# A decoder kernel on one core: decode scores in four column groups, and three half output products moved into the fourth head's attention

## Chip, core and metric

The kernel runs on one core of one Trainium2 chip. Its time is the device time of one execution in microseconds (us); shorter is better. The engines are named as in the profile: PE (TensorE matmul) and PEld (its weight loads), DVE (VectorE), ACT (ScalarE), POOL (GpSimd) and SP (SyncE, which issues most transfers). Each engine works through its own queue in order.

## What is computed

The reference is one decoder layer for a prompt of 1024 tokens and for 8 decode sequences of one new token each, whose 256 earlier keys and values lie in a paged cache. Cut to what matters:

```python
xp = xp + merge_groups(oa, o_r, gr, subln, lam_init) @ w_out      # prompt: attention and retention
# decode, for the 8 sequences:
k_past = cache_k[page_table]                                       # 2 pages of 128 keys each
k_all = concatenate([k_past, ka_d], axis=1)                        # and the new key: 257
def probs(qi, ki):                                                 # for each half of q and k
    s = einsum('bqhd,bkhd->bhqk', qi, ki) * scale + bias
    return softmax(where(mask, s, neg))
attn = probs(q1, k1) - lam * probs(q2, k2)                         # 4 heads, two softmaxes each
oa_d = einsum('bhqk,bkhd->bqhd', attn, v_all)
```

Retention, a memory attention, a squared-ReLU MLP and the norms follow or stand beside this.

## The kernel before

All float32 products of the body are made of two parts: a number is split into a high part in the type fp32r and the rest, and `mm3` issues three matmuls for each term (high by high, high by low, low by high). Activations lie transposed, 128 channels by 1032 tokens (1024 of the prompt and 8 of decode), in `UH` and `UL`, rows 0 to 7; products work on `CH` = 344 tokens at a time, so c = 0, 1, 2. Weight blocks ("units") come by one DMA of 512 KB each into a buffer `raw` and are split by ACT (high part, L128) and DVE (low part, L129).

Prompt attention runs head by head. PE's order is written out by hand there (`pin`): a loop over g = -4 to 39 whose body is a list `todo` for item g (head g // 10): `turn(g + 1)` transposes a block of probabilities (L78, then ACT `ah` L1049 and DVE `al` L1050), `scores` makes two score products for each bank (tile `sp`) which DVE adds to the mask and reduces (L1016), ACT exponentiates (L1022) and DVE combines (L1031), and `weigh(g)` multiplies by the values (tile `av`). Scores of the next head are made from its place 5 on, so from g = 33 there are none. Between the pieces of `todo` stand steps of a generator called filler: for heads 0 to 2 the projection of the next head; for the fourth head (g = 28 to 39) the decode steps, so many at each g as `DFILL` says.

`decode_steps` (from L1149) first fetches cached key pages (`fetch`, 256 KB each, two to a step; tile `ck`), builds a block-diagonal query `qblkd` and then makes 16 score products of 64 columns (4 heads x 8 sequences x 2 halves) by 512 cached keys of all four heads in tile `dsc`; `hm` picks the right head's 128 of them in eight DVE operations (L1229). A bias product (`dbias`) and the new token's own score (`down`) come between. Softmax over 64 rows, a combination product (`dcomb`, L1241) and a way through DRAM (`atd`, `at`) give the weights that the decode values need later. Twelve empty steps keep the combination behind g = 39.

`operand_steps` brings the retention half of the output projection's operand into rows 4 to 7 of UH and UL (L1266, DMAs of 2064 KB from OPH and OPL, issued by POOL), and the heads' outputs into rows 0 to 3. They are called at the g of `OPERAND_AT`. `out_ahead` begins the output projection inside the loop: at g = 37, 38 and 39 four steps each of three matmul terms' worth, the first four terms (rows 4 to 7) of the products (0,0), (0,1), (1,0), where (ft, c) is an output block of 128 channels and a third of the tokens. The remaining steps stand behind the loop. Four units of its weights are loaded at g = 32 (`LOADS_AT`) and split at the g of `UNITS_AT`.

`proj_residual` (L1439) then does the other products: for ft = 0 to 7 the first two thirds of the tokens, 24 matmuls each, DVE adding the residual from the `x` rows (L1459), ACT and POOL summing squares; then the last thirds, five of them begun (`stage`) while the decode values are finished, since these tokens include the decode ones. `fetch` there brings the x rows and weight units. The memory queries (tile `mq`) follow.

## Time and profile before

| what | value |
| --- | --- |
| time, median of 3 runs | 1483.44 us (1481.57 to 1485.17) |
| profiled execution | 1483.49 us |
| its span, first to last instruction | 1481.7 us |
| PE busy | 1468.0 us (99%), 10917 matmul records |
| DVE busy | 1097.3 us (74%) |
| ACT, POOL busy | 677.6 us (46%), 305.6 us (21%) |
| chain that ended last | PE 90%, DVE 5%, ACT 2% |
| DMA | 236.69 MB, mean 160 GB/s |

Busy time is the union of an engine's instructions. A matmul's record includes the time until its results are through, so the records of neighbouring matmuls overlap, and the distance between two starts tells what one costs. The time in brackets behind a row of the timeline is how long the engine was idle before it, and who released it. Times within the span are counted from its first instruction.

### The profile page before, as it was taken

Reading aid. Unit: us, or ns where it says so; the run is one execution under the profiler, and the core shown is the slowest. Engines: PE = TensorE matmul, PEld = TensorE weight load, DVE = VectorE, ACT = ScalarE, POOL = GpSimd, SP = SyncE. Lnnn points to the kernel's source line nnn. Section 1 sums busy time; section 2 is a strip of 40 time slices with the busy share of each in tenths; the row PEclk is TensorE's granted clock in tenths of the full one; section 3 lists DMA queues with packets and bytes.
Section 4 is the critical chain, followed back from the end, with each engine's and each line's share of the span. In section 5 each row is a group of like instructions: output and inputs, shape, how many; then the busy total and the mean of one; then the engine's idle time right before and its main releaser. Section 6 shows DMA issues by size and latency. Waiting matters only on the chain.

```text
span 1481.7 us, 27906 instructions
## 1 busy us (share of the span) xinstructions
PE 1468.0 (99%) x10917; PEld 1399.2 (94%) x10917; DVE 1097.3 (74%) x2265; ACT 677.6 (46%) x1328; POOL 305.6 (21%) x331
## 2 busy tenths in 40 slices
PE   9999999999999999999999999999999999999998
PEld 7899779999679999989999999999999999999998
DVE  7666536888768545567877987888888888787876
ACT  6534435666552341258536544333434443343454
POOL 0035333122214311106022000000001311110380
PEclk9999999999999999999999999999999999999998
DMA  8255738214846177474582443334446774536273
GB/s 288 68 187 169 205 70 190 72 34 143 253 145 242 68 247 189 118 237 109 179 299 69 157 148 131 141 137 157 158 144 211 239 252 143 172 102 194 79 130 115
DMA packets 125784, 236.69 MB, mean 160 GB/s; under 512 B 13654, under 2 KB 75787, under 8 KB 125524
## 3 DMA queue, kind: packets, MB, share of 16 engines
q1 hardware_dynamic: 90826, 174.52, 37.2%
q0 software_dynamic: 23632, 40.60, 10.2%
q10 hardware_dynamic: 11194, 19.78, 3.6%
q8 instruction: 86, 1.41, 0.4%
q14 instruction: 46, 0.38, 0.1%
HBM read 170.24 MB, written 57.52 MB: 154 GB/s over the span
## 4 chain that ended last, share of the span: by engine, by line
PE 90%; DVE 5%; ACT 2%; issue 1%; DMA 1%; ACTq 0%; POOL 0%; SPq 0%; DVEq 0%
PE dn L2345 21%; PE Z L2177 9%; PE qkp L75 7%; PE pr_o L75 6%; PE mq L75 6%; PE pr_m L75 6%; PE X L2177 6%; PE Y L2177 6%; PE grp L75 3%; PE sp L75 2%; PE av L75 2%; PE mv L75 2%; PE mk L75 1%; PE mpv L75 1%; PE vap_z L522 1%
## 5 line engine op out<-in xcount | busy, mean ns | idle before, releaser
L2345 PE MATMUL dn<-UH,wd 128*128 128x258 f32 (+1 forms) x1800 | 325.9, 283 | 0.9 <-DVE c L2479 0.8
L2345 PEld LDWEIGHTS dn<-UH,wd 128*128 128x128 f32 x1800 | 278.7, 189 | 1.8 <-DVE c L2479 0.8
L2345 PE MATMUL dn<-UL,wd 128*128 128x258 f32 x900 | 253.9, 282 | 0.0
L2345 PEld LDWEIGHTS dn<-UL,wd 128*128 128x128 f32 x900 | 169.7, 189 | 0.1
L2479 DVE TENSOR_TENSOR c<-c,dn 128x258 f32<-128x258 f32 (+1 forms) x217 | 88.8, 417 | 36.7 <-PE dn L2345 34.2
L2203 ACT ACTIVATE hq<-r 128x258 f32<-128x258 f32 x128 | 53.7, 421 | 118.0 <-DVE r L2202 117.9
L2177 PE MATMUL Z<-T_h,wu 128*128 128x258 f32 x512 | 98.1, 283 | 0.0
L2177 PE MATMUL X<-UH,wu 128*128 128x258 f32 x512 | 97.5, 282 | 0.0
L2321 ACT CAST wd<-raw_d 128x512 fp32r<-128x512 f32 x96 | 58.7, 619 | 79.6 <-PE dn L2345 74.1
L1985 ACT CAST wu<-raw_up 128x512 fp32r<-128x512 f32 x96 | 59.0, 616 | 61.0 <-PE Z L2177 53.2
L2314 ACT CAST UH<-raw_h 128x1032 fp32r<-128x1032 f32 x56 | 58.7, 1055 | 53.3 <-PE dn L2345 27.7
L2177 PEld LDWEIGHTS X<-UH,wu 128*128 128x128 f32 x512 | 81.3, 188 | 0.0
L2177 PEld LDWEIGHTS Z<-T_h,wu 128*128 128x128 f32 x512 | 81.3, 189 | 0.0
L2315 DVE TENSOR_TENSOR UL<-raw_h,UH 128x1032 fp32r<-128x1032 f32 x56 | 73.7, 1315 | 8.4 <-ACT UH L2314 8.4
L2322 DVE TENSOR_TENSOR wd<-raw_d,wd 128x512 fp32r<-128x512 f32 x96 | 72.2, 758 | 10.3 <-ACT wd L2321 10.3
L2214 POOL DMA_DIRECT2D HT<-ht x32 | 17.1, 536 | 292.0 <-DVE ht L2213 271.6
L2177 PE MATMUL Z<-T_l,wu 128*128 128x258 f32 x256 | 72.3, 282 | 0.0
L2177 PE MATMUL X<-UL,wu 128*128 128x258 f32 x256 | 72.3, 282 | 0.0
L128 ACT CAST wh_u<-raw_u 128x1024 fp32r<-128x1024 f32 x43 | 44.5, 1048 | 57.3 <-PE mq L75 36.4
L1986 DVE TENSOR_TENSOR wu<-raw_up,wu 128x512 fp32r<-128x512 f32 x96 | 64.8, 689 | 3.7 <-ACT wu L1985 3.7
L129 DVE TENSOR_TENSOR wl_u<-raw_u,wh_u 128x1024 fp32r<-128x1024 f32 x39 | 48.6, 1257 | 19.8 <-ACT wh_u L128 19.6
L75 PE MATMUL qkp<-UH,wh_u 128*128 128x344 f32 x192 | 62.8, 327 | 0.1
(606 smaller groups left out, 4657.2 us busy)
## 6 DMA issues: line engine op xcount, KB each, us to landing
raw_u<-in_wall SPq DMA_DIRECT2D x49, 512.0 KB
HT<-ht POOLq DMA_DIRECT2D x32, 516.0 KB, 3.0
raw_h<-HT SPq DMA_DIRECT2D x32, 516.0 KB
raw_up<-in_wall SPq DMA_DIRECT2D x32, 512.0 KB
raw_d<-in_wall SPq DMA_DIRECT2D x32, 512.0 KB
HQ<-hq ACTq DMA_DIRECT2D x32, 387.0 KB
raw_h<-HQ SPq DMA_DIRECT2D x24, 516.0 KB
cmk<-in_cmk SPq DMA_DIRECT2D x16, 512.0 KB
```

The source lines that it names most:

```text
L75: pinned(nc.tensor.matmul(out, l, r, start=start, stop=stop))
L129: (lo_engine or nc.vector).tensor_sub(wl[:, :n], raw[:, :n], wh[:, :n].bitcast(F32))
L1985: nc.scalar.copy(w[:, :512], src)
L1986: nc.vector.tensor_sub(w[:, 512:], src, w[:, :512].bitcast(F32))
L2177: pinned(nc.tensor.matmul(ps, l, r[:, k, :], start=first and k == 0 and x == 0, stop=k == 3 and x == 2, skip_group_check=True))
L2203: nc.scalar.activation(h[:, PLACE[quad], :], r, AF.Square)
L2314: nc.scalar.copy(h, rv)
L2315: nc.vector.tensor_sub(l, rv, h.bitcast(F32))
L2321: nc.scalar.copy(w[:, :512], src)
L2322: nc.vector.tensor_sub(w[:, 512:], src, w[:, :512].bitcast(F32))
L2345: pinned(nc.tensor.matmul(ps[:, part], l, r[:, k, cq], start=first and k == 0 and x == 0, stop=k == 3 and x == 2, skip_group_check=True))
L2479: nc.vector.tensor_add(y, y, ps)
```

## The change

Decode scores: for each of the 16 former products there are four matmuls of 16 columns (8 sequences x 2 halves of one head) by the 128 keys of that head alone, each into its own group of 32 PSUM partitions of one bank that holds all 257 scores; one step issues two of these sets of four. The bias, at half its size, opens and closes the accumulation in that bank, the new token's score comes in as one more product, and the masked additions go. Softmax reads the bank, 128 rows of which 64 count. The sixteen score steps become eight.

Half products: a new generator `half_steps` loads the first weight unit of the output projection at g = 26, splits it at g = 29, loads three blocks of x at g = 30, and in twelve steps of three matmuls makes the first four terms of the products (1,1), (0,2) and (1,2), adds the block of x to each and writes the sum to DRAM (`XH`). `PLAN` replaces `DFILL`: at each g a string of decode steps (d) and half steps (h). In `proj_residual` these three products keep only their last four terms, and their residual is read from XH in place of x. The steps of `out_ahead` are spread over g = 34 to 39, the early seven products leave out (1,1) and take in (3,1), and the last thirds that are staged are (2,2) to (6,2).

The diff, cut to its core (the `sel` constant changes its shape accordingly):

```diff
-    def mm3(out, terms, lo=0, hi=None):
-        n = len(terms)
+    def mm3(out, terms, lo=0, hi=None, n=None, first=0):
+        n = n or len(terms)
         for x, (lh, ll, rh, rl) in list(enumerate(terms))[lo:hi]:
-            mm(out, lh, rh, x == 0, False)
+            mm(out, lh, rh, x == first, False)
             mm(out, lh, rl, False, False)
             mm(out, ll, rh, False, x == n - 1)
...
+    XH = dram.tile([2, P, T], F32, tag="XH", name="XH")
...
-            sel = A.tile([64, 32], F32, tag="sel", name="sel")
-            nc.sync.dma_start(sel, i["sel"])
-            hm = A.tile([64, 5], F32, tag="hm", name="hm")
-            nc.sync.dma_start(hm, i["hm"])
-            rel64 = A.tile([32, 64], F32, tag="rel64", name="rel64")
+            SD = A.tile([P, 260], F32, tag="SD", name="SD")
+            relw = SD[:32, 0:128]
...
+            nc.vector.tensor_scalar(relw.rearrange("p (h c) -> p h c", h=4), relb.unsqueeze(2).to_broadcast([32, 4, 32]), 0.5, None, ALU.mult)
...
-            nc.gpsimd.memset(qx, 0.0)
+            prod = qk[:, 512:640]
+            nc.gpsimd.memset(qk[:, 0:640], 0.0)
...
-            prod = qk[:, 512:544]
-            nc.vector.tensor_mul(prod.rearrange("p (h s) -> p h s", h=4), qdec, kdec)
-            oneh = qk[:32, 544:801]
+                nc.vector.tensor_mul(
+                    prod[ms].rearrange("p (h c) -> p h c", h=4)[:, :, 8 * m : 8 * m + 8], qdec[ms], kdec[ms])
+            oneh = qk[:32, 640:897]
             nc.sync.dma_start(oneh, i["onehot_dec"])
-            SD = A.tile([64, 260], F32, tag="SD", name="SD")
+            sel, second = qk[:, 900:932], qk[:, 932:933]
+            nc.sync.dma_start(qk[:, 900:933], i["sel"])
...
-            def dec_bias():
-                bp = dt("dbias")
-                mm(bp[:64, :257], rel64, oneh, True, True)
-                nc.scalar.copy(SD[:, :257], bp[:64, :257])
-                yield
-                bp = dt("down")
-                for m in range(2):
-                    ms = slice(64 * m, 64 * m + 64)
-                    mm(bp[32 * m : 32 * m + 32, :1], prod[ms], ones[ms], True, True)
-                nc.vector.tensor_add(SD[:, 256:257], SD[:, 256:257], bp[:64, :1])
-                yield
+            sp = dt("dsc")
+            mm(sp[:, :257], relw, oneh, True, False)
+            mm(sp[:, 256:257], prod, ones, False, False)
+            yield
...
             for j in range(2):
-                sp = dt(f"dsc_{j}")
                 for x in range(4):
                     raw = raws2[4 * j + x]
-                    if (j, x) == (0, 2):
-                        yield from dec_bias()
                     for y in range(2):
                         q = 2 * x + y
-                        mm(sp[:64, :], qx[:, q * 64 : q * 64 + 64], raw[:, y * 512 : y * 512 + 512], q == 0, q == 7)
-                        yield
-
+                        for h in range(4):
+                            pinned(nc.tensor.matmul(
+                                sp[32 * h : 32 * h + 16, j * P : j * P + P],
+                                qx[:, q * 64 + 16 * h : q * 64 + 16 * h + 16],
+                                raw[:, y * 512 + h * P : y * 512 + h * P + P],
+                                start=False, stop=False, skip_group_check=True))
                     if 4 * j + x in (0, 1, 2, 4):
                         fetch(4 + (0, 1, 2, 0, 3)[4 * j + x])
-                sd = SD[:, j * P : j * P + P]
-                for h in range(4):
-                    nc.vector.scalar_tensor_tensor(sd, sp[:64, h * P : h * P + P], hm[:, h : h + 1], sd, ALU.mult, ALU.add)
-            mn = A.tile([64, 4], F32, tag="dmn", name="dmn")
-            nc.vector.tensor_reduce(mn[:, 0:1], SD[:, :257], AX.X, ALU.min)
-            nc.scalar.activation(SD[:, :257], SD[:, :257], AF.Exp, bias=mn[:, 0:1], scale=-1.0, accum_out=mn[:, 1:2])
+                    yield
+
+            mm(sp[:, :257], relw, oneh, False, True)
+            mn = A.tile([P, 4], F32, tag="dmn", name="dmn")
+            nc.vector.tensor_reduce(mn[:, 0:1], sp[:, :257], AX.X, ALU.min)
+            nc.scalar.activation(SD[:, :257], sp[:, :257], AF.Exp, bias=mn[:, 0:1], scale=-1.0, accum_out=mn[:, 1:2])
 
...
-            for _ in range(12):
-                yield
+            yield
             ap = dt("dcomb")
             mm(ap[:32, :257], sel, SD[:, :257], True, True)
...
-            yield from decode
...
-                    mm3(ps[:, :CH], proj_terms(us_out[:2], ft % 2, c, OUT_KT), x, x + 1)
+                    mm3(ps[:, :CH], proj_terms(us_out[:1], ft % 2, c, OUT_KT[:4]), x, x + 1, 8)
                     yield
...
+        def half_steps():
+            raw = G.tile([P, T], F32, tag="raw", name="raw_o0", bufs=3)
+            nc.sync.dma_start(raw[:, :1024], i["wall"][U_OUT])
+            raws_out.append(raw[:, :1024])
+            yield
+            with tc.issue_after(seen["ACT"]), tc.issue_after(seen["E"]):
+                us_out.append(unit(U_OUT, raw=raws_out[0]))
+            yield
+            xs = G.tile([P, T], F32, tag="rb2", name="x_half")
+            for n, (ft, c) in enumerate(OUT_HALVES):
+                nc.sync.dma_start(xs[:, n * CH : n * CH + CH], i["xT"][:, ft, c * CH : c * CH + CH])
+            yield
+            bank = PS.tile([P, 512], F32, tag="acc", name="pr_half", bufs=2)[:, :CH]
+            for n, (ft, c) in enumerate(OUT_HALVES):
+                for x in range(4):
+                    mm3(bank, proj_terms(us_out[:1], ft, c, OUT_KT[:4]), x, x + 1, 4)
+                    if x < 3:
+                        yield
+                xc = xs[:, n * CH : n * CH + CH]
+                nc.vector.tensor_add(xc, bank, xc)
+                nc.sync.dma_start(XH[ft, :, c * CH : c * CH + CH], xc)
+                yield
+
+        halves = half_steps()
+
+        def step(kind):
+            next(halves if kind == "h" else decode)
...
+            if g in HALVES_AT:
+                next(halves)
...
-            n = DFILL[g - 28] if dec else FILL - (g > 17)
+            n = len(PLAN[g - 28]) if dec else FILL - (g > 17)
+            kinds = iter(PLAN[g - 28] if dec else "")
             for y, f in enumerate(todo):
...
-                    if dec or (3, 2, 0) not in done:
+                    if dec:
+                        step(next(kinds))
+                    elif (3, 2, 0) not in done:
                         next(filler, None)
...
-                for x, nm in enumerate(("KA0", "KA1", "KB0", "KB1")):
+                for x, nm in ((1, "KA0"), (2, "KA1"), (3, "KB0")):
                     raw = A.tile([P, NT], F32R, tag=nm, name=f"raw_o{x}").bitcast(F32)
...
-        for _ in filler:
-            pass
+        for rest_of in (filler, decode, halves):
+            for _ in rest_of:
+                pass
...
-                nc.sync.dma_start(xdst(ft), xsrc(ft))
+                n = min([c for f, c in halved if f == ft], default=3) * CH
+                nc.sync.dma_start(xdst(ft)[:, :n], xsrc(ft)[:, :n])
+                if n < T:
+                    nc.sync.dma_start(xdst(ft)[:, n:], XH[ft, :, n:])
...
+        def products(ps, ft, c, lo=0, hi=None):
+            first = 4 if (ft, c) in halved else 0
+            mm3(ps[:, :CH], terms(ft, c), max(lo, first), hi, first=first)
...
-        order = [(ft, c) for ft in range(8) for c in range(2)] + [(ft, 2) for ft in range(8)]
+        order = list(early) + [(ft, c) for ft in range(8) for c in range(2) if (ft, c) not in early] + [(ft, 2) for ft in range(8)]
...
-            if (ft, c) in ((1, 1), (2, 1)):
-                fetch(ft + 1)
+            if (ft, c) in order[3:6:2]:
+                fetch(2 if (ft, c) == order[3] else 3)
...
-                mm3(ps[:, :CH], terms(ft, c), done)
+                products(ps, ft, c, done)
...
-                mm3(ps[:, :CH], terms(ft, c))
+                products(ps, ft, c)
...
-                first_rstd, ahead=len(OUT_EARLY), early=early_out, stage=([(0, 2), (1, 2)], [(2, 2), (3, 2), (4, 2)]),
+                first_rstd, ahead=len(OUT_EARLY), early=early_out, stage=([(2, 2), (3, 2)], [(4, 2), (5, 2), (6, 2)]), halved=OUT_HALVES,
...
-FILL, DFILL = 14, (1, 3, 4, 3, 1, 1, 2, 2, 1, 1, 1, 1)
+FILL = 14
+PLAN = ('d', 'ddd', 'dd', 'dhhd', 'dhh', 'dhh', 'hd', 'h', 'h', 'h', 'h', 'h')
+HALVES_AT = (26, 29, 30)
+OUT_HALVES = [(1, 1), (0, 2), (1, 2)]
...
-LOADS_AT, UNITS_AT = 32, (34, 35, 37, 38)
-OUT_EARLY = [(ft, c) for ft in range(4) for c in range(2)][:7]
-OUT_AT = {37: 4, 38: 4, 39: 4}
+LOADS_AT, UNITS_AT = 32, (35, 37, 38)
+OUT_EARLY = [(ft, c) for ft in range(4) for c in range(2) if (ft, c) not in OUT_HALVES]
+OUT_AT = {34: 1, 35: 2, 36: 2, 37: 2, 38: 3, 39: 2}
```

## Rows read from the trace of the kernel before

**Rows 1.** The page: busy time of the engines, and the granted clock.

```profile
PE 1468.0 (99%) x10917; PEld 1399.2 (94%) x10917; DVE 1097.3 (74%) x2265; ACT 677.6 (46%) x1328; POOL 305.6 (21%) x331
...
PEclk9999999999999999999999999999999999999998
```

**Rows 2.** Table by stretches: us, PE, PEld, DVE, ACT, POOL, clock, DMA share, GB/s.

```profile
387.77:395.23 7.46, 6.37 (x24) 2.82 (x23) 7.18 (x23) 5.06 (x14) 0.56 (x2) 1.00 1.13 352
395.23:407.81 12.58, 12.49 (x54) 6.21 (x52) 9.14 (x28) 6.13 (x14) 1.77 (x3) 1.00 0.91 333
407.81:436.46 28.65, 28.28 (x154) 19.25 (x152) 21.24 (x47) 17.00 (x27) 3.45 (x6) 1.00 0.56 185
436.46:528.76 92.30, 92.30 (x575) 88.25 (x575) 59.24 (x127) 31.16 (x55) 37.59 (x31) 1.00 0.42 149
```

**Rows 3.** Timeline of PE, 390 to 391.5: start, us, what, [idle before].

```profile
390.53 0.41 PE L75 MATMUL sp<-KA,Q 128*128 128x320 f32 x1 [0.86 <-DVE mn L1016]
```

**Rows 4.** Timeline of PE, 407.8 to 412.1, around one decode score product.

```profile
408.33 1.07 PE L75 MATMUL dsc<-ck,qblkd 128*64 128x512 f32 x2
409.34 0.50 PE L75 MATMUL sp<-KA,Q 128*128 128x512 f32 x1
409.68 0.40 PE L75 MATMUL sp<-KB,Q 128*128 128x512 f32 x1
409.92 0.40 PE L75 MATMUL sp<-KA,Q 128*128 128x512 f32 x1
```

**Rows 5.** Groups by line, 387.77 to 436.46: busy us, mean ns, idle.

```profile
L75 PE MATMUL dsc<-ck,qblkd 128*64 128x512 f32 x32 | 17.1, 617 | 0.0
...
L78 PE MATMUL trA<-ident,e 128*128 128x128 f32 x36 | 6.4, 281 | 0.6 <-DVE e L1031 0.6
...
L1229 DVE SCALAR_TENSOR_TENSOR SD<-dsc,hm,SD 64x128 f32<-64x128 f32 x8 | 2.7, 336 | 0.7 <-PE dsc L75 0.7
```

**Rows 6.** The chain that ended last, 388 to 470: start, us, what.

```profile
398.04 0.57 PE dbias L75 x2
...
405.05 0.91 PE av L75 x6
...
428.48 1.89 PE pr_o L75 x12
```

**Rows 7.** Timeline of PE, 207.5 to 208.8: four products in four column groups.

```profile
207.66 1.06 PE L75 MATMUL opd<-vb,hsel 128*32 128x512 f32 x8
```

**Rows 8.** Timeline of all engines, 525 to 529, where the memory queries begin.

```profile
525.62 1.22 DVE L129 TENSOR_TENSOR wl_u<-raw_u,wh_u 128x1024 fp32r<-128x1024 f32 x1
...
528.76 0.32 PE L75 MATMUL mq<-UH,wh_u 128*128 128x344 f32 x1
```

**Rows 9.** Timeline of POOL, 385 to 428.

```profile
385.41 0.80 POOL L1266 DMA_DIRECT2D UL<-OPL  x1 [0.66 <-PE qkp L75]
...
387.36 0.76 POOL L1266 DMA_DIRECT2D UH<-OPH  x1
395.02 1.64 POOL L992 TENSOR_TENSOR VL<-vraw,VH 128x512 fp32r<-128x512 f32 x1 [6.90 <-ACT VH L990]
```

**Rows 10.** The tile UH, 380 to 410: its fetch to landing.

```profile
DMA to landing us min/median/max: 19.6/19.6/19.6
```

**Rows 11.** Table by stretches, 388 to 411, columns as in rows 2.

```profile
388.00:407.00 19.00, 17.82 (x71) 8.33 (x71) 15.54 (x48) 10.97 (x27) 2.10 (x4) 1.00 1.03 357
407.00:411.00 4.00, 4.00 (x20) 2.73 (x21) 3.65 (x12) 1.72 (x3) 0.00 (x0) 1.00 0.00 0
```

**Rows 12.** Table by stretches near the end, columns as in rows 2.

```profile
1470.00:1474.00 4.00, 3.40 (x34) 3.24 (x32) 1.55 (x5) 2.75 (x9) 0.00 (x0) 1.00 0.55 187
1474.00:1476.00 2.00, 1.69 (x8) 1.38 (x7) 0.86 (x3) 0.43 (x3) 0.00 (x0) 0.57 0.00 0
```

**Rows 13.** Timeline of PE, 0 to 7, the start of the span.

```profile
1.12 4.64 PE L299 MATMUL qkp<-idle 128*128 128x128 f32 x20 [1.12 <-DVE idle L297]
...
6.62 0.40 PE L75 MATMUL qkp<-wh_u,UH 128*128 128x512 f32 x1
```

More of the change, by code (lines that the diff above doesn't have):

```diff
@@ L1186, in decode_steps @@
             qx = qk[:, 0:512]
-            nc.gpsimd.memset(qx, 0.0)
+            prod = qk[:, 512:640]
+            nc.gpsimd.memset(qk[:, 0:640], 0.0)
             for m in range(2):
-                base = qx[64 * m : 64 * m + 64, 32 * m : 32 * m + 1]
+                ms = slice(64 * m, 64 * m + 64)
+                base = qx[ms, 8 * m : 8 * m + 1]
                 nc.scalar.copy(
-                    bass.AP(tensor=base.tensor, offset=base.offset, ap=[base.ap[0], [8, 4], [65, 8]]),
-                    qdec[64 * m : 64 * m + 64],
-                )
@@ L1197, in decode_steps @@
             nc.sync.dma_start(oneh, i["onehot_dec"])
-            SD = A.tile([64, 260], F32, tag="SD", name="SD")
+            sel, second = qk[:, 900:932], qk[:, 932:933]
+            nc.sync.dma_start(qk[:, 900:933], i["sel"])
             yield
-            def dec_bias():
-                bp = dt("dbias")
-                mm(bp[:64, :257], rel64, oneh, True, True)
-                nc.scalar.copy(SD[:, :257], bp[:64, :257])
-                yield
-                bp = dt("down")
-                for m in range(2):
-                    ms = slice(64 * m, 64 * m + 64)
-                    mm(bp[32 * m : 32 * m + 32, :1], prod[ms], ones[ms], True, True)
-                nc.vector.tensor_add(SD[:, 256:257], SD[:, 256:257], bp[:64, :1])
-                yield
+            sp = dt("dsc")
@@ L1234, in decode_steps @@
+            mm(sp[:, :257], relw, oneh, False, True)
+            mn = A.tile([P, 4], F32, tag="dmn", name="dmn")
+            nc.vector.tensor_reduce(mn[:, 0:1], sp[:, :257], AX.X, ALU.min)
+            nc.scalar.activation(SD[:, :257], sp[:, :257], AF.Exp, bias=mn[:, 0:1], scale=-1.0, accum_out=mn[:, 1:2])
             nc.vector.reciprocal(mn[:, 1:2], mn[:, 1:2])
-            nc.vector.tensor_scalar(mn[:, 2:3], nlam[:64], 1.0, None, ALU.subtract)
-            nc.vector.tensor_scalar(mn[:, 2:3], mn[:, 2:3], hm[:, 4:5], 1.0, ALU.mult, ALU.add)
+            nc.vector.tensor_scalar(mn[:, 2:3], nlam, 1.0, None, ALU.subtract)
@@ L1237, in decode_steps @@
+            nc.vector.tensor_scalar(mn[:, 2:3], mn[:, 2:3], second, 1.0, ALU.mult, ALU.add)
             nc.vector.tensor_mul(mn[:, 1:2], mn[:, 1:2], mn[:, 2:3])
             nc.vector.tensor_scalar(sel, sel, mn[:, 1:2], None, ALU.mult)
-            for _ in range(12):
-                yield
+            yield
             ap = dt("dcomb")
@@ L1436, in decoder_step, with proj_residual @@
             pass
-    def proj_residual(A, bank, base, ktorder, xsrc, xdst, ssum, nm, us0, steps, when, parts, sums_done, ahead=0, early=None, stage=()):
+    def proj_residual(A, bank, base, ktorder, xsrc, xdst, ssum, nm, us0, steps, when, parts, sums_done, ahead=0, early=None, stage=(), halved=()):
         third = []
@@ L1480, in proj_residual @@
             ps, done = early[ft, c]
-            mm3(ps[:, :CH], terms(ft, c), done, 7)
+            products(ps, ft, c, done, 7)
             early[ft, c] = ps, 7
         for ft, c in order:
-            if (ft, c) in ((1, 1), (2, 1)):
-                fetch(ft + 1)
+            if (ft, c) in order[3:6:2]:
+                fetch(2 if (ft, c) == order[3] else 3)
             if (ft, c) in early:
                 ps, done = early[ft, c]
-                mm3(ps[:, :CH], terms(ft, c), done)
+                products(ps, ft, c, done)
             else:
@@ L2604, in _constants @@
     r = np.arange(64)
-    c["sel"] = (r[:, None] % 32 == np.arange(32)[None, :]).astype(f)
-    c["hm"] = np.concatenate([(r[:, None] % 32 // 8 == np.arange(4)[None, :]), r[:, None] >= 32], 1).astype(f)
+    r = np.arange(P)
+    sel = (r[:, None] // 32 * 8 + r[:, None] % 8 == np.arange(32)[None, :]) & (r[:, None] % 32 < 16)
+    c["sel"] = np.concatenate([sel, r[:, None] % 32 // 8 == 1], 1).astype(f)
     pp = np.arange(P)
```

6 lines of the change are left out of this document (2 added, 4 removed).

## The prediction, made before the change was run

> **What bounds the kernel now.** I read the page first: PE is busy for 99% of the span and its clock is granted in full in every slice [rows 1]. A busy PE need not be a fast one, since the ends of matmuls are modelled, so from here on I go by the distance between starts and by what PE waits for. The second view is a table by stretches [rows 2]. Its first three rows are the fourth head's steps g = 29 to 39 and the decode combination behind them, 48.7 us in all; the fourth is the output projection up to the first memory-query product, 92.3 us without one idle moment of PE. In the first row DVE is busy for 7.18 of 7.46 us and PE for less: PE waits there for score banks that DVE has to empty, at most 0.86 us [rows 3]. In the second row DVE still has 9.14 of 12.58 us, most of it early; from there on PE sets the pace.
>
> **What goes from PE.** A decode score product (64 weight columns by 512 moving ones, two records) takes 1.01 us from its start to the next product's, and that one is slowed by its change of mode: 0.34 to its second matmul where the next pair has 0.24 [rows 4]. I put the change of mode ahead of it at another 0.1. That makes 1.2 us, and there are 16 (32 records, [rows 5]): 19.2 us. The bias product takes 0.57 [rows 6], 0.8 with its changes of mode, the own-token product some 0.3 by the same. Together 20.3 us.
>
> **What comes to PE there.** *Scores.* Each of the 16 becomes four matmuls of 16 weight columns by 128 moving ones, in four column groups. The trace has that form at four times the length: four products of 128x32 by 512 columns take 1.06 us together [rows 7], one score product of 512 columns 1.07 [rows 4]. So four groups run abreast, and a set of four at 128 columns costs a quarter of a score product's 1.0, 0.25 us. A step is now two sets, 0.5, plus 0.2 for the changes of mode: 0.7, eight times, 5.6 us. If the groups did not run abreast, it would be 8 x 0.25 + 0.2 = 2.2; I take 0.7, since the row with the same column groups is the nearest. The bias product is issued twice (1.6), the own-token product once without a change of mode (0.1). Decode comes to 7.3 us. *Halves.* 12 matmuls of 344 columns take 1.89 us [rows 6], 0.157 each; a step "h" is three, 0.47, and there are twelve: 5.65 us. So this stretch holds 20.3 - 7.3 - 5.65 = 7.35 us less of PE work, and the output projection 36 x 0.157 = 5.65 less. If nothing waited, 13.0 us would go.
>
> **What waits.** *DVE, until about 402.* The score work of g = 29 and 30 already runs at DVE's pace. DVE loses the eight masked additions (0.34 each, [rows 5]), but only after 407, and gains the low half of the first weight unit, moved from g = 34 to 29: a subtraction of 1.22 us as in [rows 8]. So what PE saves before g = 31, some 1.5 us, mostly becomes waits, and the first "h", behind the scores (6,0) of g = 31, is reached at about 402.5 by the old trace's clock.
>
> *The operands of "h".* It multiplies rows 4 to 7 of UH and UL, which POOL fetches from OPH and OPL once the last head projection has read the old contents; the two issues are at 385.41 and 387.36 [rows 9]. The second lands 19.6 us after its issue, at 407.0 [rows 10]; the 16 DMA engines are full until then and idle right after [rows 11]. Before the change the first reader is the first output product, at 428.5 [rows 6], so this lateness cost nothing. Now PE comes at 402.5 and, its order being fixed, stands for some 5 us with the turns, scores and weighings of g = 31 and later behind it. Could the landing be later than 407.0? The change adds 512 KB of weights (g = 26) and three blocks of x (516 KB, g = 30) to SP's queue. At 357 GB/s [rows 11] that is 2.9 us, so 407.0 to 409.9. But the weights take the place in the queue that the fifth pair of key pages had, since that pair now has to wait until the second head is scaled; the sixth waits, as a pair does now, for the value buffer, and the x blocks stand behind it. Little comes in front: I take 407.5. By the Trainium skill, "Trainium Kernel Development and Optimization", section Key Constraints, transfers issued by SP, ACT and POOL share the same 16 engines and interleave; by that alone the upper end holds, and the sum would be 2.4 us worse.
>
> *After that wait.* Before the change, the weighing of g = 31 starts at 405.05 [rows 6] and the stretch ends at 436.46 [rows 2]: 31.4 us, with nine score products (10.8) and one wait of 0.6 for DVE [rows 5]. The rest, 20.0, stays; with twelve h (5.65), three score steps (2.1) and the last bias (0.8) it is 28.6. DVE has caught up during the wait. One accumulation bank serves all three half products, so the fifth and the ninth h wait for the addition before them: 0.5 us of DVE beside 2 us of other PE work. The later unit splits and gain products of ACT and DVE, 1.0 to 1.3 us each, can hold up a weighing; I allow 0.5 in all. The stretch then ends at 407.5 + 28.6 + 0.5 = 436.6, against 436.46: 0.1 us later. The 7.35 us are eaten by DVE's pace and the new wait.
>
> *Edits at nothing.* The softmax reads PSUM and is 128 rows high instead of 64, same lengths; its result is combined only after g = 39, as before. XH is written three times and read twice, 172 KB a block; the last write follows the last h and is read when SP comes to the x rows, which on its queue follow the decode weights' way through DRAM. SP stands at each XH write until DVE's addition; behind it are loads for splits at g = 35 and later, and without that cover each costs up to 0.5.
>
> *Output projection.* PE never waits in it, so its 36 matmuls come off. 24 of them (3.8 us) lie in the third columns, after the row sums are sent: the memory queries start at 525.0 instead of 528.76 on the old clock, want their second unit 1.9 us later, at 526.9, and its low half is ready at 526.84 [rows 8]. No slack is left; I charge 0.4.
>
> **Sum.** +0.1 - 5.65 + 0.4 = -5.15 us. The profiled execution took 1483.49 us (a span of 1481.7 and 1.8 around it), 0.05 above the median of the three runs. 1483.49 - 5.15 = 1478.3.
>
> **Rivals.**
> 1. *The clock falls in the wait.* No row shows a wait of 5 us in the body, and the clock falls at no shorter one. It fell once, from 2.4 to 1.2 GHz by 1474 to 1476, when PE had had only narrow matmuls and short waits [rows 12]; that speaks for a fall. Price: at the start 20 records of 128 columns took 4.64 us, 0.23 each, and full rate is there at 6.62, 5.5 us after the first [rows 13]. Half of 5.5 is the bound, 2.7; say 2.2: 1480.5. The Trainium skill, "TensorE: Matmul & The Clock Gate", section What's actually happening, calls the throttled state the default that activity lifts; by that a fall is likely if PE really stands still, and both ends of this trace agree.
> 2. *No wait at the first h.* If the fetch lands by 402.5, 4.5 to 5 us more go: 1473.6. For it: a pair of key pages leaves the queue ahead of the fetch's middle. Against: full engines until 407 [rows 11].
> 3. *The groups don't run abreast* (the change doesn't do what it says). A step is then 2.2, 1.5 more. The first five delay PE to about 408.5, which takes the place of the wait; the last three add 4.5: 1483.8.
> 4. *Slower: the fetch starts late.* On POOL's queue it stands ahead of the value subtraction, which ends at 396.7, although the program issues it behind [rows 9]. Should the new order put it behind, it lands at 396.7 + 19.6 = 416.3, 8.8 later than forecast: 1487.1, and 1489.3 with the clock's fall. It makes the kernel slower from a landing at 415.7 on. Against: its buffers come free as early as before.
>
> **How the numbers follow.** Forecast 0.42; clock 0.24; no wait 0.13; groups 0.06; late fetch 0.07; 0.08 spread. A measurement of this kernel can tell 0.2%, 3.0 us, from no change, so faster is below 1480.5: all of no wait, nine tenths of the forecast, half of the clock case, 0.03 of the rest, together 0.66. Slower: late fetch and 0.02 of the rest, 0.09. No change: 0.25. The range takes in no wait, forecast and clock with their bounds: 1473.2 to 1482.0. The forecast's own is 1476.5 to 1480.7 (landing 407.0 to 409.9).
>
> **What would show it.** Right: 128 PE records of dsc in about 5.6 us; a wait of PE of 4 to 6 us at the first half product, ended by the fetch into UH; the combination within 1.5 us of 436; 86 to 87 us from there to the memory queries. Wrong: a first half product that starts at once, a landing before 404 or after 410, sets of four over 0.35 us apart, or new waits of PE after the memory queries begin.

## The result: slower by 0.4%, and where the time went

The changed kernel takes 1490.03 us (median of 7 runs, 1484.27 to 1492.6), the kernel before 1482.45 beside it; the ratio of the means is 1.0041, 95% interval 1.0024 to 1.0057. Forecast were 1478.3 and a range up to 1482.0. The profiled execution took 1490.65 us, its span 1488.6. The seven executions differ with the clock (a mean granted clock of 0.995 in the quickest, 0.991 in the slowest), so a profile, which is one execution, is one sample of what follows.

The page of the changed kernel: busy PE, the granted clock, and the engines' shares of the chain that ended last.

```profile
PE 1462.8 (98%) x11013; PEld 1404.0 (94%) x11013; DVE 1101.1 (74%) x2259; ACT 677.3 (46%) x1327; POOL 305.3 (21%) x331
...
PEclk9999999999999999999999999999999999999999
...
PE 56%; DVE 3%; DMA 2%; ACT 1%; issue 1%; DVEq 0%; POOL 0%; SPq 0%; ACTq 0%; POOLq 0%
```

PE is busy for 5.2 us less than in [rows 1], as a change that takes work away should show, and the span is 6.9 us longer. The clock's digits look untouched, but a slice is 37 us and the digit 9 stands for 90% and more, so a few microseconds at half rate don't show in it. Nor can the chain's shares be set beside the 90% for PE before: here they add up to some 63%, not 99%, because the chain, followed back from the end, breaks off at 541.4 us (its first lines stand below). One has to go to the stretches. The next table is cut where the stages and the clock change (us, then PE, PEld, DVE, ACT, POOL, granted clock, DMA share, GB/s):

```profile
386.90:390.90 4.00, 1.17 (x6) 0.49 (x4) 3.89 (x11) 2.15 (x7) 0.35 (x1) 1.00 1.15 335
390.90:397.72 6.82, 6.82 (x50) 4.99 (x49) 2.83 (x13) 4.18 (x10) 0.00 (x0) 0.50 1.11 402
397.72:407.28 9.56, 6.67 (x75) 4.71 (x74) 7.57 (x18) 3.42 (x8) 2.15 (x3) 1.00 1.03 381
407.28:437.84 30.56, 29.42 (x234) 26.02 (x233) 22.96 (x53) 17.99 (x30) 3.54 (x6) 1.00 0.51 166
437.84:526.32 88.48, 86.87 (x540) 82.52 (x539) 59.45 (x130) 31.11 (x56) 37.08 (x31) 1.00 0.45 159
526.32:564.98 38.66, 36.88 (x226) 34.87 (x226) 13.64 (x26) 11.93 (x20) 2.52 (x5) 1.00 0.82 204
564.98:571.80 6.82, 5.07 (x18) 5.07 (x19) 4.69 (x22) 2.48 (x3) 0.38 (x2) 0.50 0.47 137
```

Lines 2 and 7 are the find: the granted clock is 0.50, 1.2 GHz, for 6.8 us each. (A third such stretch, 3.4 us, lies at 783 us.) In the kernel before, PE ran at 2.4 GHz from 6.6 to 1474 us. Against [rows 2], by the starts of the same instructions:

| stretch | before | after | difference | forecast |
| --- | --- | --- | --- | --- |
| ahead of g = 29 | 387.77 | 386.90 | -0.9 | 0 |
| g = 29 to the combination | 48.69 | 50.94 | +2.3 | +0.1 |
| output projection | 92.30 | 88.48 | -3.8 | -5.25 |
| from the memory queries to the end | 952.9 | 962.3 | +9.3 | 0 |

So the largest part of the loss lies where the change edits nothing. An estimate from this trace accounts for 8.4 of these 9.3 us: 3.5 of waits at the repeated query rows, 2.5 for the fall at 565 us (half of PE's 5.07 busy us), 1.7 for the one at 783 us and 0.7 more of waits at a later transpose (0.9 against 0.2). What PE waited for, in the attention and around the memory queries (us in total, times, longest):

```profile
PE dsc L75 <- DMA qblkd<-in_onehot_dec: 2.7, 1, 2.7
PE trA L78 <- DVE e L1032: 1.5, 3, 0.7
PE dsc L1210 <- DMA ck<-in_cache_kT: 1.2, 1, 1.2
PE av L75 <- DVE VL L993: 1.0, 1, 1.0
PE av L75 <- DVE al L1051: 0.5, 1, 0.5
...
PE rep_m L864 <- DVE dex_m L863: 3.5, 2, 2.2
PE mq L75 <- DVE x L1488: 1.2, 1, 1.2
```

The first: the bias product now opens the accumulation and so stands at g = 29, one item earlier than before, while the one-hot table it multiplies stands on SP's queue behind the new load of the weight unit and arrives at 390.4. The clock falls 0.5 us after that wait. The wait forecast at the first half product is not in the list. PE's timeline shows why:

```profile
399.17 0.63 PE L1210 MATMUL dsc<-ck,qblkd 128*16 128x128 f32 x16
399.73 0.44 PE L75 MATMUL sp<-KA,Q 128*128 128x384 f32 x1
...
404.44 0.41 PE L1210 MATMUL dsc<-ck,qblkd 128*16 128x128 f32 x8
406.03 0.41 PE L1210 MATMUL dsc<-ck,qblkd 128*16 128x128 f32 x8 [1.19 <-DMA ck<-in_cache_kT]
...
407.28 0.32 PE L75 MATMUL pr_half<-UH,wh_u 128*128 128x344 f32 x1
```

PE reached that product at 407.28 (forecast 407.5), and UH had landed 1.1 us earlier; three other late things had held PE up until then. The same rows confirm the four column groups: the four matmuls of one set (eight records) take 0.41 us to their end, and a step of two sets that nothing holds up takes 0.56 us from its start to the next product's. All 128 records of dsc are busy for 6.1 us, a part of them at half rate.

Past 526 us, the chain (start, us, what) of the changed kernel:

```profile
541.42 2.84 issue
...
545.00 10.68 DMA rrow<-rm
...
556.19 6.68 DMA raw_u<-in_wall
...
562.97 1.05 ACT wh_u L128
...
565.19 0.83 DVE qm L1740 x2
...
566.74 0.69 PE rep_m L864 x2
```

The reciprocal norms of the memory rows go through DRAM in 10.7 us; SP waits for them to read them back, and behind that read stands a weight unit of the memory queries. Its low half is made by DVE ahead of the scaled queries (qm) from which PE makes the repeated rows (rep_m). SP's queue before the change, then after it (start, us, what), tells where this comes from:

```profile
525.52 0.34 SPq L122 DMA_DIRECT2D raw_u<-in_wall  x1
...
526.87 0.33 SPq L122 DMA_DIRECT2D raw_u<-in_wall  x1
...
532.60 2.48 SPq L122 DMA_DIRECT2D raw_u<-in_wall  x2
...
535.61 0.90 SPq L1638 DMA_DIRECT2D memT<-in_memT  x2
...
565.73 0.34 SPq L1656 DMA_DIRECT2D rmb<-rrow  x1
```

```profile
527.51 0.42 SPq L122 DMA_DIRECT2D raw_u<-in_wall  x1
...
529.41 0.84 SPq L1667 DMA_DIRECT2D memT<-in_memT  x2
...
531.20 1.01 SPq L122 DMA_DIRECT2D raw_u<-in_wall  x1
...
545.93 0.46 SPq L122 DMA_DIRECT2D raw_u<-in_wall  x1
...
555.75 0.34 SPq L1685 DMA_DIRECT2D rmb<-rrow  x1
556.19 9.44 SPq L122 DMA_DIRECT2D raw_u<-in_wall  x4
```

Before, all the weight units that are wanted soon go out ahead of the memory rows; after, three of them go behind. Nobody wrote this order: where instructions are not pinned, the program's scheduler orders each queue. Among the kernels here in which nothing pins these loads, the new order stands in every profile with shortened third columns and the old one in every profile with whole ones; what in the change moved it was not tested.

**Theory.** W: PE's removed work was cover. Without it PE waits for things that were late all along, the clock falls behind such waits, and each fall costs about as much as the wait. W2: past 526 us the loss comes from the order of loads there. Rivals: the narrow products themselves lower the clock; the full DMA engines make everything late in any order; earlier arrival alone makes the waits.

### The profile page after: what moved, and what is told of

Same layout as the page of the kernel before. It is cut to its first block, busy times and chain, and to the rows that moved or that the text cites. A ratio compares the mean times of both kernels' runs of the same rounds, so it can differ in the third digit from the quotient of the medians.

```text
span 1488.6 us, 28100 instructions
## 1 busy us (share of the span) xinstructions
PE 1462.8 (98%) x11013; PEld 1404.0 (94%) x11013; DVE 1101.1 (74%) x2259; ACT 677.3 (46%) x1327; POOL 305.3 (21%) x331
## 4 chain that ended last, share of the span: by engine, by line
PE 56%; DVE 3%; DMA 2%; ACT 1%; issue 1%; DVEq 0%; POOL 0%; SPq 0%; ACTq 0%; POOLq 0%
PE dn L2374 19%; PE Z L2206 9%; PE pr_m L75 6%; PE X L2206 6%; PE Y L2206 6%; PE mq L75 4%; PE mv L75 1%; PE mk L75 1%; PE mpv L75 1%; PE ms L75 1%; DMA rrow<-rm 1%; DMA raw_h<-HT 1%; DVE UL L2344 0%; DMA raw_u<-in_wall 0%; PE mtr L78 0%
## 5 line engine op out<-in xcount | busy, mean ns | idle before, releaser
L75 PE MATMUL mq<-UH,wh_u 128*128 128x344 f32 x192 | 62.5, 326 | 1.2 <-DVE x L1488 1.2
```

What stands on the lines that cost most here:

```text
L75: pinned(nc.tensor.matmul(out, l, r, start=start, stop=stop))
```

## Experiments

The first number behind each expectation is the median, then comes the ratio of the means to the kernel before run beside it, whose median was 1482.5 to 1483.0 us, with its 95% interval.

**The one-hot table first.**

```diff
-HALVES_AT = (26, 29, 30)
+HALVES_AT = (29, 30, 31)
```

> The first half steps (load of the first output weight unit, its split, the x blocks) come at g = 29, 30, 31 instead of 26, 29, 30, so that on SP's queue the bias constants (one-hot and selection) stand ahead of that load. Theory W (the changed kernel loses by new waits of PE and by the clock that falls with them): the first bias product no longer waits for the one-hot constants until 390.4 us; what ends its wait is the own-token product of DVE, ready at 389.3, so at most 1.7 us of the 2.8 us wait stay, and the half-rate clock of 390.9 to 397.7 us (3.4 us of work) goes or starts later: 1.1 to 4.5 us off the changed kernel's 1490.0, 1485.5 to 1489. Rival (the one-hot load is late because of the value load ahead of it, not because of the weight unit): it lands at about 390 as before, time within 0.5 of 1490.

1490.24 us, ratio 1.0052 (1.0038 to 1.0066): no gain. The wait for the table fell from 2.7 to 1.4 us (1.2 are left even in the kernel without any such load, below, so only about half of it came from the load; the rest comes from the earlier place of the bias), but PE then waited 1.8 for DVE's combination, and 0.5 and 1.7 for the fifth pair of key pages. Neither theory had this: the rival was wrong about the landing, W about the time. A mended wait hands over to the next late thing.

**Filling that one wait.**

```diff
+            for _ in range(18):
+                mm(sp[:, :CH], UH[:, 0, :P], UH[:, 1, :CH], True, True)
             mm(sp[:, :257], relw, oneh, True, False)
```

> 18 products of 128 x 344 (0.157 us each, 2.8 us) whose result nobody reads stand ahead of the first bias product, where PE waits 2.8 us for the one-hot constants. Nothing else changes. Theory W: the clock falls at 390.9 because PE stood still, so it stays at 2.4 GHz until the next wait, and the 6.8 us at half rate cost 3.4 us: time 1486 to 1487.5, with the first bias product still at about 390.4. Rival (the clock falls for the narrow products of the bias and of the scores, not for the wait): the half-rate stretch stays where it is, time 1490 +- 0.5.

1490.8 us, 1.0064 (1.005 to 1.0077). Two stretches of this kernel, columns as in the table above:

```profile
386.90:404.36 17.46, 12.79 (x133) 9.89 (x131) 14.30 (x43) 10.56 (x26) 2.59 (x4) 1.00 1.11 384
404.36:411.19 6.83, 5.31 (x25) 4.73 (x26) 1.53 (x6) 1.14 (x2) 0.00 (x0) 0.50 0.62 224
```

and PE's timeline:

```profile
403.73 0.41 PE L1212 MATMUL dsc<-ck,qblkd 128*16 128x128 f32 x8 [4.26 <-DMA ck<-in_cache_kT]
```

W's mechanism held: with the place filled, the bias and the narrow products of g = 29 and 30 ran at 2.4 GHz, so the rival falls. Its time did not: PE came sooner to the key pages, waited 4.3 us there instead of 1.2, and the clock fell behind that wait. The weight unit has taken the place of the fifth pair of key pages in the ring of raw buffers, so these go out 6.5 us later than before (390.1 and 383.5); the next experiment gives the place back.

**The weight unit in another ring.** With the order of the first experiment:

```diff
-            raw = G.tile([P, T], F32, tag="raw", name="raw_o0", bufs=3)
+            raw = G.tile([P, 1024], F32R, tag="wl", name="raw_o0", bufs=RING).bitcast(F32)
```

> As e1_onehot_first, and the first output weight unit comes into a buffer of the ring of split weights instead of the ring of three raw buffers, so that the fifth to eighth pairs of key pages find their places as in the kernel before. Theory W: the waits of 0.6 and 1.9 us for the fifth pair of key pages (404 and 406 us in e1) go; PE then waits for the fetch of UH and UL at the first half product, 2 to 4 us until about 407, or less if DVE's pace holds it. Against e1 (1490.2) 0.5 to 3 us less: 1487 to 1489.7; the memory stage stays as late as there. Rival (the engines are full until 407 whatever is issued, so the pages land as late): waits for the key pages of 1.5 us or more stay, time 1489.5 to 1491.

1488.99 us, 1.004 (1.0026 to 1.0054): the waits for key pages are gone, so it was their late issue and not the full DMA engines alone that made them late, and now the wait that the prediction named appears, 3.1 us until the fetch of UH lands at 407.2.

**The same, and the memory rows by ACT.** First ACT alone, on the changed kernel:

```diff
-        nc.sync.dma_start(rrow[1:2, :256].rearrange("a (t p) -> p (a t)", p=P), rm)
+        nc.scalar.dma_start(rrow[1:2, :256].rearrange("a (t p) -> p (a t)", p=P), rm)
...
-        nc.sync.dma_start(rmb, bcast_rows(rrow[1:2, :], P, 256))
+        nc.scalar.dma_start(rmb, bcast_rows(rrow[1:2, :], P, 256))
```

> Two transfers of the memory stage, the memory rows' reciprocal norms to DRAM and back to all partitions, are issued by ACT instead of SP. Theory W2 (behind these, SP holds back weight units for 10 us, whose split on DVE stands ahead of the scaling of the queries that PE waits for): the waits of 1.5 and 2.4 us at 563 and 566 us shrink to 1.5 or less together, and the clock does not fall at 565: 2.4 to 6 us off, 1484 to 1487.6. Rival (what is late is the norm row itself, its way through DRAM lands at 560.3 because the 16 DMA engines are full): both waits stay within 1 us and the time within 1 of 1490.

1485.91 us, 1.002 (1.0009 to 1.003), 4.1 off: one wait of 1.6 us is left at the repeated rows and the clock holds there. Then both edits:

> e7_unit_apart and e2_rows_by_act together. If the two losses are separate ones, the time is that of e7 less the 4.1 us that the second brought (1490.0 to 1485.9): 1483 to 1485.5. If a gain in the one stage is lost again in the other (PE arrives earlier at the rows of the memory queries and waits longer), it is that of e2 or of e7, 1486 to 1489.

1487.94 us, 1.0039 (1.0025 to 1.0053): the second case. The waits at the repeated rows were back, 2.9 us in two, and the clock fell at 566.9. In the attention, the wait of the prediction in full, and the clock's fall with it:

```profile
408.33 0.62 PE L75 MATMUL pr_half<-UH,wh_u 128*128 128x344 f32 x1 [5.27 <-DMA UH<-OPH]
```

So the two gains don't add up. PE comes to the repeated rows half a microsecond earlier than with the rows by ACT alone (563.9 against 564.4), which doesn't explain the whole difference; the order itself had to be tested, from both sides.

**The order of loads, undone and imposed.** In the changed kernel, the memory rows' loads are issued on SP behind the sixth weight unit of the memory queries, and the first memory keys behind them:

```diff
             us = [unit(U_MQ + 2 * pr + x) for x in range(2)]
+            if pr == 2:
+                memory_rows()
...
+            with behind("SP"):
+                nc.sync.dma_start(g_mkv, i["g_mkv"])
...
-                for _ in range(3 if pr == 3 else 1):
+                for _ in range((0, (f, c) == (0, 0), 1, 3)[pr]):
```

> The changed kernel with the loads of the memory stage in the order of the kernel before: six weight units of the memory queries first, then the memory rows, then the first cached memory keys. Nothing else changes. Theory W2: the waits of 1.5 and 2.4 us at the repeated query rows and the fall of the clock at 565 us go, worth 3.9 and up to 3.4 us: 1482.5 to 1486. Rival (the rows are late because PE and DVE come to them earlier and the norm row takes its time): the waits stay, 1489 to 1491.

1483.01 us, 0.9997 (0.9988 to 1.0006): 7.0 us off. From the memory queries on, PE is not idle for a moment and the clock holds:

```profile
527.85:600.00 72.15, 72.15 (x453) 70.50 (x454) 36.41 (x95) 18.53 (x27) 8.37 (x11) 1.00 0.67 192
```

The other way round, in a kernel without this loss (column groups alone, filled, 1477.5 us; told below):

```diff
             us = []
             for x in range(2):
+                n = {3: 0, 4: 2, 5: 3}.get(2 * pr + x)
+                with nullcontext() if n is None else tc.issue_after(ahead_of[n]):
                     us.append(unit(U_MQ + 2 * pr + x))
```

> The kernel of e6_groups_filled (1477.5 us, no wait of PE over 0.1 us between 524 and 600 us) with one edit: in the memory stage three weight units of the memory queries (the 4th, 5th and 6th) are issued on SP behind the memory rows' loads, behind the reciprocal norms' way to DRAM and behind its way back, which is the order of the changed kernel. Theory W2 (what the changed kernel loses past 526 us it loses by this order): the repeated query rows come late, PE waits 2 to 4 us at them and the clock may fall: 1480.5 to 1485. Rival (the order matters only together with the third columns that are shortened, which bring PE there earlier): within 1.5 of 1477.5.

1486.23 us, 1.0025 (1.0016 to 1.0034), 8.7 more, above the expected range by 1.2. PE's waits from 520 to 570 us, and the clock:

```profile
PE rep_m L864 <- DVE dex_m L863: 4.0, 2, 2.3
```

```profile
561.34:568.17 6.83, 5.25 (x19) 5.25 (x20) 4.52 (x22) 2.48 (x3) 0.38 (x2) 0.50 0.41 124
```

That kernel has no half products and its third columns are whole. The order alone makes a loss of this size, and the rival (that it takes the shortened third columns too) falls.

**Column groups alone.** No half products, the projection and its loads as before; decode steps as in the changed kernel:

```diff
-PLAN = ('d', 'ddd', 'dd', 'dhhd', 'dhh', 'dhh', 'hd', 'h', 'h', 'h', 'h', 'h')
-HALVES_AT = (26, 29, 30)
-OUT_HALVES = [(1, 1), (0, 2), (1, 2)]
+PLAN = ('d', 'ddd', 'dd', 'dd', 'd', 'd', 'd', '', '', '', '', '')
+HALVES_AT = ()
+OUT_HALVES = []
```

> Only the decode scores in four column groups are kept; no half products, the output projection and its weight loads as in the kernel before. Theory W: 13.0 us of PE work go from g = 29 to the combination; the bias products move to g = 29 as in the changed kernel and may wait up to 1.7 us for the own-token product there, DVE's pace takes another 1.5, a fall of the clock up to 3.4, and some of the rest is taken by loads that are not there earlier: 4 to 9 us faster than before, 1473.5 to 1478.5. The memory stage has the order of loads of the kernel before and no new wait at 560. Rival 1 (the four groups do not run abreast, so the scores save nothing): within 2 us of before, 1480.5 to 1484.5. Rival 2 (the loss past 526 us comes from earlier arrival at the memory queries, not from the order of loads there): waits at the repeated query rows of 3 us or more appear here too and take back all but 2 us.

1483.22 us, 1.0004 (0.9994 to 1.0014): PE work that was forecast at 13 us is gone and nothing is gained. It looks like the first rival, but the eight matmuls of a step do take 0.56 us in its timeline. The stretches say what took the rest:

```profile
386.50:391.11 4.61, 3.15 (x28) 1.73 (x26) 4.50 (x14) 2.78 (x10) 0.38 (x1) 1.00 1.17 372
391.11:394.53 3.42, 3.42 (x34) 2.46 (x25) 1.92 (x9) 2.30 (x6) 0.21 (x1) 0.50 1.08 405
394.53:408.18 13.65, 10.62 (x125) 8.02 (x124) 11.91 (x34) 7.71 (x16) 1.41 (x3) 1.00 0.96 347
408.18:411.59 3.41, 3.41 (x12) 2.94 (x12) 2.38 (x7) 0.93 (x2) 0.00 (x0) 0.50 0.72 219
411.59:418.42 6.83, 5.02 (x44) 3.57 (x43) 5.67 (x13) 6.38 (x12) 0.56 (x3) 1.00 0.90 327
418.42:428.66 10.24, 9.91 (x45) 9.91 (x46) 7.11 (x13) 5.59 (x8) 2.70 (x3) 0.50 0.20 69
```

Waits of 6.6 us (4.4 of them for DVE's combination of the exponentials, the end of a way from scores over DVE, ACT and DVE back to PE) and 17 us at 1.2 GHz, with PE busy for all but 0.3 of them: up to half of that, some 8, is lost.

**Column groups alone, filled.** To tell waits and clock apart, the same kernel gets 47 products that nobody reads, 7.4 us, where PE stood:

```diff
+WARM = {(30, 0): 8, (32, 0): 14, (35, 0): 8, (35, 1): 8}
...
+            warm(9)
             mm(sp[:, :257], relw, oneh, True, False)
...
+                if (g, y) in WARM:
+                    warm(WARM[g, y])
                 f()
```

> The kernel of e5_groups_alone with 47 products of 128 x 344 (0.157 us each, 7.4 us) whose result nobody reads, at the five places where PE stood still there: 9 ahead of the first bias product (wait 1.38 us), 8 ahead of the turn of g = 30 (1.22), 14 ahead of that of g = 32 (2.14), 8 ahead of that of g = 35 (1.30) and 8 ahead of the weighing of g = 35 (1.24). Theory W: the 13 us of PE work that the column groups remove covered waits for the chain of scores, exponential and combination; without it PE waits 7.3 us, and the clock falls behind these waits for 17 us in all, worth some 5 to 8 us. With the places filled the clock stays at 2.4 GHz and the time comes to 1475 to 1478.5. Rival (the clock falls because of the narrow products of 16 columns, not because PE stands still): the half-rate stretches stay and the time is within 1.5 of 1483.2. Rival 2 (no cover is missing; the fill costs what it holds): 1488 or more.

1477.52 us, 0.9966 (0.9952 to 0.9979): more work, and 5.7 us less than without it. This is the fastest version, faster than both kernels. The stage, then the projection, then the memory queries:

```profile
387.45:431.70 44.25, 43.00 (x372) 35.86 (x370) 36.18 (x89) 27.67 (x53) 5.36 (x10) 1.00 0.77 273
431.70:523.91 92.21, 92.21 (x574) 88.13 (x575) 59.46 (x127) 31.17 (x55) 37.41 (x31) 1.00 0.42 150
523.91:570.00 46.09, 46.09 (x291) 44.69 (x290) 20.78 (x59) 14.74 (x25) 3.92 (x7) 1.00 0.80 219
```

44.25 us where [rows 2] have 48.7, at the full clock throughout. Without its unused products (7.6 us by their starts) and 1.0 us of waits the stage holds 35.7 us; before, without 1.4 us of waits, it held 47.3. So the column groups take some 11.6 us of PE work away, not 13.0. (The profiled execution took 1480.2 us.) The narrow score products are the same as in the kernel unfilled, so in this stage they don't lower the clock by themselves; the places where PE stood still do.

**Filled at the last two places only.**

```diff
-WARM = {(30, 0): 8, (32, 0): 14, (35, 0): 8, (35, 1): 8}
+WARM = {(35, 0): 8, (35, 1): 8}
-            warm(9)
```

> The kernel of e5_groups_alone (1483.2 us) filled only ahead of the turn and of the weighing of g = 35 (8 products of 128 x 344 each), the last two of the five places of e6. Theory W (each fall of the clock belongs to the wait ahead of it): the 10.2 us at half rate from 418 to 428 us go, worth up to 5 us; those at 391 and 408, 3.4 us each, stay: 1478.5 to 1480.5, against 1477.5 with all five places filled. Rival (the falls come from the whole stage's lower load, so a fill at its end does not keep the clock): 1482 or more, or the half-rate stretch moves to another place.

1479.89 us, 0.9981 (0.9971 to 0.9991), as W has it. In the profiled execution (1476.85 us) the fall at 391 was there and that at 418 gone; the one at 408 was gone too, though the wait ahead of it, 2.0 us, was not. Not every such wait is followed by a fall.

**A half product as filling.** In place of the last eight unused products, four half steps of (1,1), their weight unit split at g = 34 (the x row of that block then comes in three loads):

```diff
-WARM = {(30, 0): 8, (32, 0): 14, (35, 0): 8, (35, 1): 8}
+WARM = {(30, 0): 8, (32, 0): 14, (35, 0): 8}
-PLAN = ('d', 'ddd', 'dd', 'dd', 'd', 'd', 'd', '', '', '', '', '')
+PLAN = ('d', 'ddd', 'dd', 'dd', 'd', 'd', 'd', 'hhhh', '', '', '', '')
-OUT_HALVES = []
+OUT_HALVES = [(1, 1)]
```

> The kernel of e6_groups_filled (1477.5 us) with the eight unused products ahead of the weighing of g = 35 replaced by the half product (1,1), 12 matmuls in four steps at g = 35 and 36, its weight unit loaded and split where the kernel before does it. Three more matmuls' worth than the fill it replaces stand in the attention, 4 x 0.157 = 0.6 us, and 1.9 us leave the projection. Theory W (PE work is worth its length once the clock holds): 1476.2, within 1475 to 1477.5. Rival (the split of the weight unit at g = 34 is not ready when the first half step comes): a wait of 1 us or more there and a fall of the clock, 1478 to 1481.

1480.76 us, 0.9992 (0.9982 to 1.0001): the rival. PE waited 1.2 us for the unit's high part and 0.7 for its low part, and the clock was at 1.2 GHz from 418.4 to 421.8.

**All of it.** The changed kernel with the table first, the unit in the other ring, the loads as before, 31 unused products at the early places and the half steps from g = 33 on:

```diff
-PLAN = ('d', 'ddd', 'dd', 'dhhd', 'dhh', 'dhh', 'hd', 'h', 'h', 'h', 'h', 'h')
+PLAN = ('d', 'ddd', 'dd', 'dd', 'd', 'dhh', 'dhhh', 'hhh', 'h', 'h', 'h', 'h')
+WARM = {(30, 0): 8, (32, 0): 14}
```

> Column groups and all three half products, with every loss found so far mended: one-hot constants ahead of the weight unit, that unit in a buffer of the split weights' ring, 31 unused products of 128 x 344 at the three early places of e6 (9, 8, 14), the half steps at g = 33 to 39 behind the landing of UH and UL, and the memory stage's loads in the order of the kernel before. By e6 (1477.5): 5.65 us of products leave the projection, the half steps put 5.65 in place of 2.5 us of unused products: 1477.5 - 2.5 = 1475; 1473 to 1477 if the clock holds. If the fetch of UH and UL or the key pages are late again and the clock falls behind them: 1478 to 1483.

1488.41 us, 1.0028 (1.0017 to 1.0039), worse than its parts. The memory stage was mended (no wait at the repeated rows). In the attention the sixth pair of key pages, issued at 390.3 as in the filled kernel (390.0), landed later than there, with the weight unit and the x blocks, 1 MB, in flight beside it, and PE waited 0.7 and 1.5 us; a half step waited 2.0 us for the addition that empties the only bank of the halves, and the clock fell at both places, and once more at 782 us; ahead of the memory stage PE also waited 1.4 us at the row sums. Twelve half steps pushed into fewer places bring their own waits. A version in which all three half products pay was not found.

## Why the prediction was wrong

- **What goes and what comes on PE**: near. A step of two sets of four was put at 0.7 and takes 0.56; rival 3 is out. The column groups take away some 11.6 us, put at 13.0. The work removed is real, but its value was not its length: alone it brought nothing (1.0004).
- **"So what PE saves before g = 31, some 1.5 us, mostly becomes waits"**, and behind it that PE sets the pace: mis-sized. In the kernel without halves the chain over DVE and ACT makes PE wait at g = 30, 32 and 35 as well. The 16 score products were the cover of that chain, and an engine at 99% says nothing about which of its work is cover.
- **"Little comes in front" on SP**: failed. The prediction looked only at what the new load does to the fetch of UH and UL, not at who stands behind it on SP. That was the one-hot table, wanted one item earlier than before, which cost 2.7 us of waiting (about half of it by the load, the rest by the earlier place alone); and that the fifth pair of key pages loses its place was written down without asking when PE reads them, 1.2 us.
- **The wait at the first half product**: lateness right, place wrong. UH lands 19.7 us after its issue, at 406.2, and PE gets to the product at 407.28; other waits had used up the time, so that 407.28 lies near the 407.5 of the forecast is chance. Once these were taken away, 3.1 to 5.3 us appeared there. Rivals 2 and 4 (the fetch early, or late behind POOL's queue) did not happen.
- **Rival 1, the clock**: the mechanism came, at the wrong place and too small. It was tied to a wait of 5 us because no shorter one was followed by a fall; here it fell behind 2.7, and in the kernel with groups alone behind 1.2. The prediction's own [rows 12] showed a fall behind narrow matmuls and short waits, and it drew on them only for the long wait. The Trainium skill, "TensorE: Matmul & The Clock Gate", section A second HAM failure mode: psum-queue depth-cycling, describes a PE that stands still only briefly between groups of matmuls and whose clock swings nevertheless; the 17 us at 1.2 GHz behind five waits of at most 2 us agree with it.
- **Output projection**: -3.8 us in place of -5.25. The 36 matmuls left, but the start of the memory queries costs 1.2 us and not 0.4: it was not the second weight unit that was late there but DVE, which empties the last bank behind five low halves of the operand.
- **Everything past the memory queries at nothing**: failed, and the dearest, 9.3 us. The prediction shifted the old trace along with PE. But the queues there are ordered by the program's scheduler, and its order changed. Undoing that order alone brings 7.0 of the 7.6 us between the medians of the two kernels; imposing it on another costs 8.7. The text had named new waits behind the memory queries as a sign of error, without a price or a chance for them.
- **Two slips of the working**, both small: one of the two waits that make 0.6 us in [rows 5] lies ahead of g = 31 (0.18 at 388 us), so the rest holds 0.4; and a landing at 407.0 gives 1477.8 as the lower end of the forecast's own range, not 1476.5, for which the text has no working, as it has none for 1482.0.

## What to carry to other kernels

Before taking work from a busy engine, ask what waits it covers, and look at the wait that each later instruction would have without it; work that goes from a covered place is worth little until something useful stands in its stead, and where PE then stands still for one or two microseconds at a time, the clock can take more than the wait. Where a scheduler orders what is not pinned, compare the order of every queue behind the edit, also in stages that the diff does not touch, and pin the loads that are wanted first.

## What the runs showed of the hardware

The granted clock fell to 1.2 GHz behind waits of 1.2 to 5.3 us, each time for 3.4, 6.8 or 10.2 us, and filling the places with products that nobody reads kept it at 2.4: 47 such products made a kernel 5.7 us faster. It did not fall behind every such wait (1.3 us at 528 us in the kernel with the loads as before, 2.0 at 406 in the kernel filled late), so the price of a wait is a range, estimated from these rows: its length alone, or its length and half of the stretch at 1.2 GHz, 1.7 to 5 us.

It also fell where PE hardly stood still. In four profiles it fell at 426 to 428 us for 3.4 us; this is PE's timeline in the changed kernel with the loads as before, then the stretch:

```profile
423.48 0.39 PE L75 MATMUL av<-al,VH 128*128 128x256 f32 x1 [0.48 <-DVE al L1051]
...
424.17 1.84 PE L75 MATMUL ct<-ones,sq 128*128 128x1 f32 x16
```

```profile
426.30:429.71 3.41, 3.41 (x15) 3.35 (x15) 2.83 (x4) 1.20 (x2) 2.20 (x1) 0.50 0.04 13
```

Ahead of it stand one wait of 0.48 us and sixteen records of one column each, and the profile of the changed kernel has both there at 2.4 GHz throughout. In three profiles, that of the changed kernel among them, it fell at 782 to 783 us for 3.4 us, behind a wait of 0.26 us and sixteen records of eight columns, which the kernel before has too, without a fall. So a fall can follow very narrow products with short waits as well as one long wait; how much each weighs was not tested.
